# Delta-rule inverses ordered behind weight splits on DVE, and gates taken out of PSUM with one operation per head

## The chip, the cores and the metric

One core of a Trainium2 chip runs the kernel. Its engines work side by side, each through its own queue in order, and they meet through semaphores: PE (TensorE, matmuls out of SBUF into PSUM), DVE (VectorE), ACT (ScalarE), POOL (GpSimd), and SP, which here issues most DMAs. The metric is the time of one execution on the device in microseconds (us), the median of several.

## The reference: a decoder layer with two token mixers

The input x is 256 tokens by 2048 channels, in 32-bit floats. The layer is

```python
h = rmsnorm(x, norm_mix_w)
q, k, v, z, b_raw, a_raw, p_in, g_a, g_b = split(h @ w_in)
q, k, v = split(silu(causal_dwconv(concat(q, k, v), conv_qkv_w)))   # q, k l2-normalised per head
o = gated_delta_rule(q, k, v, g_log, beta)                          # 16 heads of 128, in chunks
y_a = rmsnorm(o, gdn_norm_w) * silu(z)
y_b = (causal_multiscale_pool(p_in) @ pool_w) * pool_scale
x = x + (sigmoid(g_a) * y_a + sigmoid(g_b) * y_b) @ w_out
h = rmsnorm(x, norm_ffn_w)
gate, up = split(h @ w_up)
x = x + (gelu(causal_dwconv(gate, conv_ffn_w) + conv_ffn_b) * up) @ w_down
y = rmsnorm(x, norm_final_w)
```

In the delta rule each chunk solves a unit lower triangular system, (I + L) u = rhs, with L made of products of the keys, decays and beta. The kernel uses chunks of 128 tokens, two per head, and inverts I + L.

## The kernel before

**Weights.** All weights (some 300 MB) stream through once, in tiles of 256 by 512 that are listed beforehand in `srcs` and taken in that order. `load` issues a tile's DMA on SP into one of four `raw` buffers. `begin` splits it into two parts that PE multiplies at its fast 32-bit rate: ACT casts `whi` (L141), DVE subtracts to get `wlo` (L149), three buffers each. `weights()` hands out the next tile and makes sure that the splits of the two tiles after it are in the program too (AHEAD = 2). `gemm_a` (L168) multiplies with one tile after another: for each, 12 matmuls of 512 columns (L179 high by high, L180 low by high, L181 high by low, for two halves of the tile and two blocks of tokens), into a `psm` buffer of PSUM. After each half tile it calls `side()`, which runs one step of a generator of side work. At its second tile it first runs what waits in the list `later`.

**The mixers, group by group.** The loop at L836 runs over four groups of four heads. Each multiplies in turn with K, Q, V, P (pooling input), GB (gate of the pooling branch), two tiles of pool, Z (the silu gate) and GA (gate of the delta branch); K, Q, V, P, GB, Z and GA have 8 tiles each. Group 0's K is done by hand earlier. In the second tile of V the generator `gdn` (L625) is started for the group. Its parts, with their yields:

- decays and their masks (4 yields); keys by keys and queries by keys, with the sums for the norms, giving `ga0` and `ga1` (8 yields);
- the 32 by 32 blocks on the diagonal of L go out by DMA to DRAM (`cdd`, L703) and come back spread over all partitions as `lb` (L706; 1 yield);
- WAIT = 5 empty yields, then a copy of the identity to `tb` (L715) and the inverse of all blocks, 31 columns with two dependent DVE operations each (L718, L720), a yield after every third column. Below, this is the chain of the inverse;
- `tb` goes to DRAM and back as the blocks of `TTa` (L725, L728); then what is left of `conv`, the convolution of the values (L594 to L600); ACT scales the values (L734);
- `qx`, `qp`: sums over the squared queries (L737, L740); transposes of the blocks (L745); the blocks are joined to 64 and 128 (U, px; L758 to L787); then products with the values: `w1`, `pr`, `w2` and the outputs `po`, two PSUM banks of the `psg` buffers, of which there are four (L793 to L811);
- the norm of the outputs: `pn` spreads the sums of the queries by a matmul (L814), four small DVE operations bring it to `ro` (L824); squares and sums of `po` (L819, L820); a power on POOL (L827); a factor (L829); and `on` = `po` times `ro` (L832), handed on in `res`.

At the end of a group `gated` (L901) runs the generator dry, multiplies `on` into `sz`, the product of the gates (L903), and adds `yb`, the pooling branch (L904). `mixed` (L913) transposes `sz` on PE (L224) and splits it into `mhi` (ACT, L916) and `mlo` (DVE, L917), the left side of the output projection. Groups 0 to 2 do `mixed` in the next group's K. Group 3 has its own order: 6 tiles of each of the first two column blocks of `w_out` are multiplied first, with what the groups 0 to 2 gave (`early`, L927); then come `gated` and `mixed`, and then the rest of the projection.

**What sets the order.** The program text gives each instruction its place. A planner then orders each engine's instructions with a clock of its own: an engine that is free takes, of the instructions that are ready by that clock, the one earliest in the text. So an instruction whose inputs are there early can run long before its place in the text, and one whose inputs come late in that clock is passed by others. On the chip each engine then goes through its order strictly, and waits at an instruction whose inputs are late in fact, with everything behind it. `tc.issue_after(ins)` forces what is inside to stand behind `ins` on the same engine.

Of the kernel before, what the change touches and what calls it, by code (L numbers as in the profile page):

```python
# [7 lines left out]
F32 = mybir.dt.float32  # L8
# [3 lines left out]
ALU = mybir.AluOpType  # L12

P = 128
# [6 lines left out]
EPS = 1e-6  # L21
# [6 lines left out]
NR = P // B0  # L28
AHEAD = 2
WAIT = 5  # L30


@with_exitstack
def kernel(
# [20 lines left out]
    nc = tc.nc  # L55
    mm = nc.tensor.matmul
# [10 lines left out]
    def nm(s):  # L67
        cnt[0] += 1
        return f"{s}_{cnt[0]}"

    def pg(shape=(P, 512)):
        return psg.tile(list(shape), F32, tag="g", name=nm("psg"))
# [33 lines left out]

    loads = []
    last_load = [None]
    HALVES = 2

    def weights(ahead=AHEAD):
# [21 lines left out]
    def begin(n):  # L133
        while len(made) < min(len(srcs), n):
            load(len(made) + 1)
            raw = loads[len(made)]
            shape = list(raw.shape)
            keep = kept.get(len(made))
            hi = wpool.tile(shape, F32R, tag="whi", name=nm("whi")) if keep is None else \
                mtile(keep, shape, F32R, nm("khi"))  # L140
            nc.scalar.copy(hi, raw)  # L141
            if shape[1] == 8:
                lo = None
                nc.vector.tensor_tensor(hi[:, :, 32:64], raw[:, :, 0:32], hi[:, :, 0:32].bitcast(F32),
                                        op=ALU.subtract)
            else:
                lo = wpool.tile(shape, F32R, tag="wlo", name=nm("wlo")) if keep is None else \
                    mtile(4 + keep, shape, F32R, nm("klo"))
                nc.vector.tensor_tensor(lo, raw, hi.bitcast(F32), op=ALU.subtract)  # L149
            made.append((hi, lo))  # L150


# [96 lines left out]
    mp = mix.__enter__()  # L249
# [66 lines left out]
    with tc.manual_schedule(engines={mybir.EngineType.PE, mybir.EngineType.DVE, mybir.EngineType.Activation}):  # L316
# [4 lines left out]
        n = 0  # L321
        for c in range(HALVES):
            for k in range(2):
# [108 lines left out]
    idb = mp.tile([P, 8, B0], F32, name="idb")  # L432
    for cq in range(4):
        pr = slice(32 * cq, 32 * cq + 32)
# [8 lines left out]
    for g, w in enumerate(WINDOWS):  # L443
# [11 lines left out]
    sel = mp.tile([P, 4, 32], F32, name="sel")  # L455
    nc.vector.tensor_reduce(sel[:, 0, :], ident.rearrange("p (b i) -> p i b", b=4), axis=mybir.AxisListType.X,
                            op=ALU.add)
# [4 lines left out]
    for c in range(2):  # L462
        hi, lo = weights()
# [161 lines left out]
    def gdn(g, kq, vt, conv, res):  # L625
# [6 lines left out]
        dec0 = mp.tile([P, 4, S], F32, tag="dec0", name=nm("dec0"))  # L632
# [31 lines left out]
        for hp in range(2):  # L664
            h0 = 2 * hp
            hs = slice(h0, h0 + 2)
            grams = []
            for h in (h0, h0 + 1):
# [5 lines left out]
                for t, src in ((0, pg0[:, 0:P]), (1, pg1[:, 0, :])):  # L674
                    nc.vector.tensor_tensor_reduce(jk, src, ident, scale=1.0, scalar=0.0, op0=ALU.mult,
                                                   op1=ALU.add, accum_out=ssk[:, t, h : h + 1])
# [6 lines left out]
            for h in (h0, h0 + 1):  # L683
# [4 lines left out]
                                               op0=ALU.mult, op1=ALU.mult)  # L688
# [3 lines left out]
                                               op0=ALU.mult, op1=ALU.mult)  # L692
# [15 lines left out]

        q2 = kq[:, :, 1, :]
        nc.scalar.activation(q2, q2, AF.Square)  # L710
        for _ in range(WAIT):
            yield
        tb = mp.tile([P, 8, B0], F32, tag="tb", name=nm("tb"))
        tmp = mp.tile([P, 8, B0], F32, tag="tmp", name=nm("tmp"))
        nc.vector.tensor_copy(tb, idb)  # L715
        for j in range(B0 - 1):
            tv = tmp[:, :, j + 1 :]
            nc.vector.tensor_tensor(tv, lb[:, j, j + 1 :].unsqueeze(1).to_broadcast([P, 8, B0 - 1 - j]),  # L718
# [13 lines left out]
        for h in range(4):  # L732
            for t in range(2):
# [5 lines left out]
        qp = mp.tile([P, 32], F32, tag="qp", name=nm("qp"))  # L739
        nc.vector.tensor_reduce(qp, qx.rearrange("p h (c j) -> p (h c) j", j=32), axis=mybir.AxisListType.X,  # L740
                                op=ALU.add)
        yield
        for r in range(NR):
            rs = slice(B0 * r, B0 * (r + 1))
            nc.vector.transpose(Ta[rs, :, rs], TTa[rs, :, rs])  # L745
# [27 lines left out]
        lo, up = slice(0, 64), slice(64, 128)  # L773
# [22 lines left out]
        pr = pg([P, 4, P])  # L796
# [9 lines left out]
        po = [pg([P, 4, P]) for t in range(2)]  # L806
# [3 lines left out]
            mm(po[1][:, h, :], ga0[:, h, 384:512], w1[:, h, :], start=True, stop=False)  # L810
            mm(po[1][:, h, :], ga1[:, h, P : 2 * P], w2[:, h, :], start=False, stop=True)  # L811
        yield
        pn = pg([P, 4, 2, 4])
        mm(pn.rearrange("p h t c -> p (h t c)"), sel.rearrange("p b i -> p (b i)"), qp, start=True, stop=True)  # L814
        ro = mp.tile([P, 2, 4], F32, tag="ro", name=nm("ro"))
        so = mp.tile([P, 2, 4], F32, tag="so", name=nm("so"))
        for t in range(2):
            o2 = mp.tile([P, 4, P], F32, tag="dec1", name=nm("o2"))
            nc.scalar.activation(o2, po[t], AF.Square, scale=float(P) ** -0.5)  # L819
            nc.vector.tensor_reduce(so[:, t, :], o2, axis=mybir.AxisListType.X, op=ALU.add)  # L820
        yield
        for c in range(4):
            pr = slice(32 * c, 32 * c + 32)
            nc.vector.tensor_scalar(ro[pr], pn[pr, :, :, c].rearrange("p h t -> p t h"), EPS * P, EPS * EPS * P,  # L824
                                    op0=ALU.mult, op1=ALU.add)
        nc.vector.tensor_tensor(ro, ro, so, op=ALU.add)
        nc.gpsimd.tensor_tensor(ro, ro, epsx[:, 0:1].unsqueeze(2).to_broadcast([P, 2, 4]), op=ALU.pow)  # L827
        for t in range(2):
            nc.vector.tensor_scalar(ro[:, t, :], ro[:, t, :], rsq[:, t : t + 1], None, op0=ALU.mult)  # L829
        on = mp.tile([P, 2, 4, P], F32, tag="dec0", name=nm("on"))  # L830
        for t in range(2):
            nc.vector.tensor_tensor(on[:, t], po[t], ro[:, t, :].unsqueeze(2).to_broadcast([P, 4, P]), op=ALU.mult)  # L832
        yield
        res.append(on)

    for g in range(4):  # L836
        kq = mp.tile([P, 4, 2, S], F32, tag="kq", bufs=1, name=nm("kq"))
# [7 lines left out]
        res = []  # L845
# [41 lines left out]
        tb = gate(gemm_a(xh, xl, KD), "th")  # L887
        ps = gemm_a(lambda k, t: phi[:, k, t * P : (t + 1) * P], lambda k, t: plo[:, k, t * P : (t + 1) * P], 4)
        yb = mp.tile([P, 2, 512], F32, tag="yb", name=nm("yb"))
# [4 lines left out]
        sz = mp.tile([P, 2, 512], F32, tag="sz", name=nm("sz"))  # L894
# [5 lines left out]

        def gated(sz=sz, res=res, yb=yb):  # L901
            drain()
            nc.vector.tensor_tensor(sz, res[0].rearrange("p t h d -> p t (h d)"), sz, op=ALU.mult)  # L903
            nc.vector.tensor_tensor(sz, sz, yb, op=ALU.add)  # L904

        if g < 3:
            gated()
# [31 lines left out]
    for c in range(4):  # L939
# [9 lines left out]
        for k2 in range(2):  # L949
# [5 lines left out]
            for kk in range(2):  # L955
# [4 lines left out]
                                               op0=ALU.mult, op1=ALU.subtract)  # L960
# [134 lines left out]
```

## Time and profile before

| | us |
|---|---|
| median of 3 runs | 1572.16 (1571.49 to 1575.03) |
| profiled execution | 1572.57 |
| its span, first to last instruction | 1570.8 |
| mixers, groups 0 to 3, end of Q/K of group 0 to the end of GA | 36 to 730 |
| output projection | 730 to 830 |
| gated MLP, first product | 830 to 1330 |
| its second product and the end | 1330 to 1570.8 |

TensorE's granted clock was 0.998 over the span. Timeline rows below have the start in us, the length in us, the engine, the line, the operation, what it writes and reads with shapes, how many are merged, and in brackets the idle time of the engine just before with what ended it. Rows of the page's groups have the line, the operation, shapes and count, then busy us and the mean ns of one, then idle time before them. Rows of waits have who waited for whom, the total us, how often, and the longest. A stretch's row has its length, then for PE, weight loads, DVE, ACT and POOL the busy us with the count, then clock, DMA share and GB/s.

### The profile page before, as it was taken

The page shows a single profiled execution, that of the slowest core. Times are in us where ns is not written, and L with a number is a line of the kernel's source. Part 1 is how long each engine was busy: PE and PEld are TensorE (multiplying, and loading weights), DVE is VectorE, ACT ScalarE, POOL GpSimd, SP SyncE. Part 2 cuts the span into 40 slices and gives each one's busy share as a digit, 9 for nine tenths or more (in the row PEclk, how much of TensorE's full clock was granted, in tenths as well). Part 3 has the DMA queues.
Part 4 walks back from the last instruction along what each step waited for, and adds up shares of the span by engine and source line. Part 5 has one row for each costly group of instructions (what it writes and reads, how often), then busy time and mean ns, then how long its engine had stood idle before and what let it go on. Part 6 is the DMA issues. An engine that isn't in the chain of part 4 may idle for free.

```text
span 1570.8 us, 21247 instructions
## 1 busy us (share of the span) xinstructions
PE 1558.3 (99%) x8022; PEld 1308.1 (83%) x8022; DVE 1077.4 (69%) x1647; ACT 744.7 (47%) x956; POOL 47.4 (3%) x69
## 2 busy tenths in 40 slices
PE   9999999999999999999999999999999999999997
PEld 8878888888887888888888888888888888888886
DVE  6897849796797758796656667766666667444444
ACT  6554446444554445544454544444444445334443
POOL 2110000000010001000000000000000000000000
PEclk9999999999999999999999999999999999999999
DMA  8676747666666756775555556555555566556662
GB/s 272 199 219 194 207 148 218 201 207 176 183 211 185 210 159 192 214 205 177 198 191 183 188 189 190 188 189 187 187 189 188 188 188 216 198 190 208 203 223 90
DMA packets 168229, 304.23 MB, mean 194 GB/s; under 512 B 19234, under 2 KB 22834, under 8 KB 167998
## 3 DMA queue, kind: packets, MB, share of 16 engines
q1 hardware_dynamic: 165104, 297.84, 61.0%
q10 hardware_dynamic: 3022, 5.03, 0.9%
q8 instruction: 63, 1.03, 0.3%
q14 instruction: 40, 0.33, 0.1%
HBM read 297.56 MB, written 5.27 MB: 193 GB/s over the span
## 4 chain that ended last, share of the span: by engine, by line
PE 50%; issue 1%; ACT 0%; DVE 0%; POOLq 0%; POOL 0%
PE psm L203 10%; PE psg L203 10%; PE psg L204 5%; PE psm L204 5%; PE psg L1008 2%; PE psg L1010 2%; PE psg L1009 2%; PE psm L1010 2%; PE psm L1008 2%; PE psm L1009 2%; PE psm L180 1%; PE psm L181 1%; PE psm L179 1%; PE psg L954 0%; ACT xt L1037 0%
## 5 line engine op out<-in xcount | busy, mean ns | idle before, releaser
L149 DVE TENSOR_TENSOR wlo<-raw,whi 128x1024 fp32r<-128x1024 f32 x522 | 636.9, 1222 | 379.2 <-ACT whi L141 373.6
L141 ACT CAST whi<-raw 128x1024 fp32r<-128x1024 f32 x524 | 550.8, 1053 | 715.1 <-PE psm L180 305.7
L181 PE MATMUL psm<-wlo,xhl 128*128 128x512 f32 x864 | 340.3, 394 | 1.1 <-DVE wlo L149 1.1
L179 PE MATMUL psm<-whi,xhl 128*128 128x512 f32 x864 | 339.6, 393 | 0.0
L180 PE MATMUL psm<-whi,xhl 128*128 128x512 f32 x864 | 338.2, 391 | 0.0
L203 PE MATMUL psm<-fhl,whi 128*128 128x512 f32 x704 | 246.2, 396 | 0.0
L203 PE MATMUL psg<-fhl,whi 128*128 128x512 f32 x704 | 238.0, 394 | 0.0
L204 PE MATMUL psm<-fhl,wlo 128*128 128x256 f32 x704 | 194.4, 279 | 0.0
L181 PEld LDWEIGHTS psm<-wlo,xhl 128*128 128x128 f32 x864 | 162.3, 188 | 34.8 <-DVE wlo L149 1.9
L180 PEld LDWEIGHTS psm<-whi,xhl 128*128 128x128 f32 x864 | 162.3, 188 | 33.2
L179 PEld LDWEIGHTS psm<-whi,xhl 128*128 128x128 f32 x864 | 162.3, 188 | 33.0 <-issue 0.5
L204 PE MATMUL psg<-fhl,wlo 128*128 128x256 f32 x704 | 178.7, 279 | 0.0
L203 PEld LDWEIGHTS psm<-fhl,whi 128*128 128x128 f32 x704 | 131.4, 188 | 30.5
L203 PEld LDWEIGHTS psg<-fhl,whi 128*128 128x128 f32 x704 | 129.2, 188 | 24.2
L204 PEld LDWEIGHTS psg<-fhl,wlo 128*128 128x128 f32 x704 | 132.5, 188 | 6.9
L204 PEld LDWEIGHTS psm<-fhl,wlo 128*128 128x128 f32 x704 | 132.5, 188 | 1.1
L1008 PE MATMUL psg<-whi,hhi 128*128 128x512 f32 x168 | 65.5, 390 | 0.0
L1008 PE MATMUL psm<-whi,hhi 128*128 128x512 f32 x168 | 65.4, 389 | 0.0
L1009 PE MATMUL psm<-whi,hlo 128*128 128x512 f32 x168 | 65.4, 389 | 0.0
L1010 PE MATMUL psm<-wlo,hhi 128*128 128x512 f32 x168 | 65.4, 389 | 0.0
L1009 PE MATMUL psg<-whi,hlo 128*128 128x512 f32 x168 | 65.4, 389 | 0.0
L1010 PE MATMUL psg<-wlo,hhi 128*128 128x512 f32 x168 | 59.1, 389 | 0.0
(263 smaller groups left out, 1527.2 us busy)
## 6 DMA issues: line engine op xcount, KB each, us to landing
raw<-in_w_in_dram SPq DMA_DIRECT2D x224, 512.0 KB, 4.2
raw<-in_w_up_dram SPq DMA_DIRECT2D x176, 512.0 KB, 4.6
raw<-in_w_down_dram SPq DMA_DIRECT2D x88, 512.0 KB, 4.3
raw<-in_w_out_dram SPq DMA_DIRECT2D x32, 512.0 KB, 3.7
mv<-vrow SPq DMA_DIRECT2D x12, 512.0 KB, 5.8
taps<-in_conv_qkv_w_dram SPq DMA_DIRECT2D x16, 256.0 KB, 5.6
raw<-in_pool_w_dram SPq DMA_DIRECT2D x8, 512.0 KB, 5.3
vrow<-ev SPq DMA_DIRECT2D x4, 512.0 KB, 3.1
```

Source lines behind the costliest of these rows:

```text
L141: nc.scalar.copy(hi, raw)
L149: nc.vector.tensor_tensor(lo, raw, hi.bitcast(F32), op=ALU.subtract)
L179: mm(ps[:, t, :], lh(k, t), hi[:, kk, :], start=(k == 0), stop=False)
L180: mm(ps[:, t, :], ll(k, t), hi[:, kk, :], start=False, stop=False)
L181: mm(ps[:, t, :], lh(k, t), lo[:, kk, :], start=False, stop=(k == nk - 1))
L203: mm(ps[f], hi[:, kk, fs], rhl(k), start=(k == 0), stop=False, skip_group_check=True)
L204: mm(ps[f][:, 1, :], lo[:, kk, fs], rhl(k)[:, 0, :], start=False, stop=(k == nk - 1), skip_group_check=True)
L1008: mm(acc[c][t], lh(k, t), hi[:, kk, :], start=(k == 0), stop=False)
L1009: mm(acc[c][t], ll(k, t), hi[:, kk, :], start=False, stop=False)
L1010: mm(acc[c][t], lh(k, t), lo[:, kk, :], start=False, stop=(k == KF - 1))
```

## The change

Three things are done. The copy that opens the inverse is put behind the newest weight split that the text has made at that point (`last_split`), and comes 26, 24, 22 or 18 calls of `side()` later in the text, by group, with all of the generator that follows it. The matmul `pn` and its four operations move from behind `po` to behind `qp`. And `on` is gone: `gated` multiplies `po` in PSUM into `sz` (two operations), then for each of eight pairs of head and token block one operation multiplies by the factor `ro` and adds `yb`.

```diff
@@ -28,6 +28,7 @@
 NR = P // B0
 AHEAD = 2
 WAIT = 5
+LATE = (26, 24, 22, 18)
 
 
 @with_exitstack
@@ -106,6 +107,7 @@
 
     loads = []
     last_load = [None]
+    last_split = [None]
     HALVES = 2
 
     def weights(ahead=AHEAD):
@@ -146,7 +148,7 @@
             else:
                 lo = wpool.tile(shape, F32R, tag="wlo", name=nm("wlo")) if keep is None else \
                     mtile(4 + keep, shape, F32R, nm("klo"))
-                nc.vector.tensor_tensor(lo, raw, hi.bitcast(F32), op=ALU.subtract)
+                last_split[0] = nc.vector.tensor_tensor(lo, raw, hi.bitcast(F32), op=ALU.subtract).ins
             made.append((hi, lo))
 
 
@@ -708,11 +710,13 @@
 
         q2 = kq[:, :, 1, :]
         nc.scalar.activation(q2, q2, AF.Square)
-        for _ in range(WAIT):
+        for _ in range(WAIT + LATE[g]):
             yield
         tb = mp.tile([P, 8, B0], F32, tag="tb", name=nm("tb"))
         tmp = mp.tile([P, 8, B0], F32, tag="tmp", name=nm("tmp"))
-        nc.vector.tensor_copy(tb, idb)
+
+        with tc.issue_after(last_split[0]):
+            nc.vector.tensor_copy(tb, idb)
         for j in range(B0 - 1):
             tv = tmp[:, :, j + 1 :]
             nc.vector.tensor_tensor(tv, lb[:, j, j + 1 :].unsqueeze(1).to_broadcast([P, 8, B0 - 1 - j]),
@@ -740,6 +744,13 @@
         nc.vector.tensor_reduce(qp, qx.rearrange("p h (c j) -> p (h c) j", j=32), axis=mybir.AxisListType.X,
                                 op=ALU.add)
         yield
+        pn = pg([P, 4, 2, 4])
+        mm(pn.rearrange("p h t c -> p (h t c)"), sel.rearrange("p b i -> p (b i)"), qp, start=True, stop=True)
+        ro = mp.tile([P, 2, 4], F32, tag="ro", name=nm("ro"))
+        for c in range(4):
+            pr = slice(32 * c, 32 * c + 32)
+            nc.vector.tensor_scalar(ro[pr], pn[pr, :, :, c].rearrange("p h t -> p t h"), EPS * P, EPS * EPS * P,
+                                    op0=ALU.mult, op1=ALU.add)
         for r in range(NR):
             rs = slice(B0 * r, B0 * (r + 1))
             nc.vector.transpose(Ta[rs, :, rs], TTa[rs, :, rs])
@@ -810,28 +821,18 @@
             mm(po[1][:, h, :], ga0[:, h, 384:512], w1[:, h, :], start=True, stop=False)
             mm(po[1][:, h, :], ga1[:, h, P : 2 * P], w2[:, h, :], start=False, stop=True)
         yield
-        pn = pg([P, 4, 2, 4])
-        mm(pn.rearrange("p h t c -> p (h t c)"), sel.rearrange("p b i -> p (b i)"), qp, start=True, stop=True)
-        ro = mp.tile([P, 2, 4], F32, tag="ro", name=nm("ro"))
         so = mp.tile([P, 2, 4], F32, tag="so", name=nm("so"))
         for t in range(2):
             o2 = mp.tile([P, 4, P], F32, tag="dec1", name=nm("o2"))
             nc.scalar.activation(o2, po[t], AF.Square, scale=float(P) ** -0.5)
             nc.vector.tensor_reduce(so[:, t, :], o2, axis=mybir.AxisListType.X, op=ALU.add)
         yield
-        for c in range(4):
-            pr = slice(32 * c, 32 * c + 32)
-            nc.vector.tensor_scalar(ro[pr], pn[pr, :, :, c].rearrange("p h t -> p t h"), EPS * P, EPS * EPS * P,
-                                    op0=ALU.mult, op1=ALU.add)
         nc.vector.tensor_tensor(ro, ro, so, op=ALU.add)
         nc.gpsimd.tensor_tensor(ro, ro, epsx[:, 0:1].unsqueeze(2).to_broadcast([P, 2, 4]), op=ALU.pow)
         for t in range(2):
             nc.vector.tensor_scalar(ro[:, t, :], ro[:, t, :], rsq[:, t : t + 1], None, op0=ALU.mult)
-        on = mp.tile([P, 2, 4, P], F32, tag="dec0", name=nm("on"))
-        for t in range(2):
-            nc.vector.tensor_tensor(on[:, t], po[t], ro[:, t, :].unsqueeze(2).to_broadcast([P, 4, P]), op=ALU.mult)
-        yield
-        res.append(on)
+        yield
+        res.append((po, ro))
 
     for g in range(4):
         kq = mp.tile([P, 4, 2, S], F32, tag="kq", bufs=1, name=nm("kq"))
@@ -900,8 +901,14 @@
 
         def gated(sz=sz, res=res, yb=yb):
             drain()
-            nc.vector.tensor_tensor(sz, res[0].rearrange("p t h d -> p t (h d)"), sz, op=ALU.mult)
-            nc.vector.tensor_tensor(sz, sz, yb, op=ALU.add)
+            po, ro = res[0]
+            for t in range(2):
+                nc.vector.tensor_tensor(sz[:, t, :], po[t].rearrange("p h d -> p (h d)"), sz[:, t, :], op=ALU.mult)
+            for t in range(2):
+                for h in range(4):
+                    hs = slice(h * P, (h + 1) * P)
+                    nc.vector.scalar_tensor_tensor(sz[:, t, hs], sz[:, t, hs], ro[:, t, h : h + 1], yb[:, t, hs],
+                                                   op0=ALU.mult, op1=ALU.add)
 
         if g < 3:
             gated()
```

## The prediction

> **What bounds the kernel now.** First the busy shares of the page, then the waits of PE.
>
> ```profile
> span 1570.8 us, 21247 instructions
> PE 1558.3 (99%) x8022; PEld 1308.1 (83%) x8022; DVE 1077.4 (69%) x1647; ACT 744.7 (47%) x956; POOL 47.4 (3%) x69
> ```
> ```profile
> PE psm L181 <- DVE wlo L149: 2.1, 2, 1.1
> PE psm L240 <- POOL ones L230: 1.1, 1, 1.1
> PE psm L180 <- DVE mlo L917: 0.6, 1, 0.6
> PE psm L179 <- ACT mhi L916: 0.5, 1, 0.5
> ```
>
> PE sets the time: its idle time is 1570.8 - 1558.3 = 12.5 us, and its recorded waits for other engines are 4.3 us in five pieces. One (1.1 us) is the start. The other four are all that work on DVE and ACT can give back: two waits for a weight split (L149) and two where the last group's gated values enter the output projection (L916, L917). So the question is whether the change takes away these four, and whether it makes others. The next view is PE's timeline at the four.
>
> ```profile
> 136.01 0.39 PE L179 MATMUL psm<-whi,phi 128*128 128x512 f32 x1
> 136.24 0.39 PE L180 MATMUL psm<-whi,plo 128*128 128x512 f32 x1
> 137.64 0.50 PE L181 MATMUL psm<-wlo,phi 128*128 128x512 f32 x1 [1.01 <-DVE wlo L149]
> ...
> 491.80 0.39 PE L180 MATMUL psm<-whi,xhl 128*128 128x512 f32 x1
> 493.30 0.50 PE L181 MATMUL psm<-wlo,xhl 128*128 128x512 f32 x1 [1.11 <-DVE wlo L149]
> ...
> 769.96 1.03 PE L224 MATMUL psg<-ident,sz 128*128 128x128 f32 x8
> 771.51 0.74 PE L179 MATMUL psm<-whi,mhi 128*128 128x512 f32 x2 [0.52 <-ACT mhi L916]
> 772.89 0.50 PE L180 MATMUL psm<-whi,mlo 128*128 128x512 f32 x1 [0.64 <-DVE mlo L917]
> 773.23 0.39 PE L181 MATMUL psm<-wlo,mhi 128*128 128x512 f32 x1
> ```
>
> The starts say more than the busy time: undisturbed, one 512-column matmul starts 0.23 us after the one before (136.01 to 136.24), so a weight tile of 12 matmuls takes PE about 2.72 us; I call that a step. At 137.64 the start is 137.64 - 136.24 - 0.23 = 1.17 us late, at 493.30 it is 1.27 us late. At the junction behind the transposes (L224) the waits are 0.52 us and then 773.23 - 771.51 - 3 x 0.23 = 1.03 us. [...]
>
> **What makes the two splits late.** DVE and ACT around these places:
>
> ```profile
> 128.90 1.23 DVE L149 TENSOR_TENSOR wlo<-raw,whi 128x1024 fp32r<-128x1024 f32 x1 [0.92 <-ACT whi L141]
> 136.03 0.42 DVE L718 TENSOR_TENSOR tmp<-lb,tb 128x248 f32<-128x248 f32 x1 [5.91 <-DMA lb<-cdd]
> 136.37 1.22 DVE L149 TENSOR_TENSOR wlo<-raw,whi 128x1024 fp32r<-128x1024 f32 x1
> ...
> 484.46 1.23 DVE L149 TENSOR_TENSOR wlo<-raw,whi 128x1024 fp32r<-128x1024 f32 x1 [0.69 <-ACT whi L141]
> 491.69 0.42 DVE L718 TENSOR_TENSOR tmp<-lb,tb 128x248 f32<-128x248 f32 x1 [6.00 <-DMA lb<-cdd]
> 492.02 1.22 DVE L149 TENSOR_TENSOR wlo<-raw,whi 128x1024 fp32r<-128x1024 f32 x1
> ```
> ```profile
> 130.54 1.05 ACT L141 CAST whi<-raw 128x1024 fp32r<-128x1024 f32 x1 [1.68 <-PE psm L180]
> 133.26 1.05 ACT L141 CAST whi<-raw 128x1024 fp32r<-128x1024 f32 x1 [1.67 <-PE psm L180]
> ...
> 486.10 1.05 ACT L141 CAST whi<-raw 128x1024 fp32r<-128x1024 f32 x1 [1.68 <-PE psm L180]
> ```
>
> In groups 0 and 2 the first product of the inverse (L718) stands on DVE in front of a split and waits 5.91 and 6.00 us until lb has landed. The cast that the split needs was done at 131.59 and 487.15, but the split runs at 136.37 and 492.02. In groups 1 and 3 the same wait is shorter and PE shows nothing:
>
> ```profile
> 313.33 0.42 DVE L718 TENSOR_TENSOR tmp<-lb,tb 128x248 f32<-128x248 f32 x1 [4.62 <-DMA lb<-cdd]
> ...
> 660.76 1.23 DVE L149 TENSOR_TENSOR wlo<-raw,whi 128x1024 fp32r<-128x1024 f32 x1 [1.42 <-ACT whi L141]
> 667.14 0.42 DVE L718 TENSOR_TENSOR tmp<-lb,tb 128x248 f32<-128x248 f32 x1 [3.60 <-DMA lb<-cdd]
> ```
>
> So DVE may stand still for 4.62 us and PE notices nothing; at 5.91 us it costs 1.17. That is the slack against which every new wait on DVE is held.
>
> **The change part by part.**
>
> *The tie (L715).* The copy that opens the inverse now follows the newest split. Which one that is comes from counting yields. Before the copy lie 4 + 8 + 1 yields and then 5 + LATE, so the copy is reached in call 14 + 5 + LATE: 45, 43, 41, 37. V's product gives 14 calls (the generator starts at its second tile), P's 16, GB's 16 at two per tile. So the copy is reached in tile 7, 6, 5 and 3 of GB. Splits are made two tiles ahead, so the tie is to the split of pool tile 1, pool tile 0, GB tile 7, GB tile 5. Counting the L149 rows by tile, the last split ahead of the first L718 is now GB 7, GB 6, GB 6, GB 5. The tie thus moves two, two, one and no splits in front of the chain.
>
> Group 0: the split of pool 0 can run from 131.59 to 132.8 and that of pool 1 from 133.26 + 1.05 = 134.31 to 135.5; the copy (292 ns) ends at 135.8 and L718 finds lb at 136.03. Both splits fit in the time that DVE stood still, and the chain starts no later. The 1.17 us go. Group 2: GB 7's split runs from 487.15 to 488.4 and L718 then waits until 491.69, 3.3 us, under the 4.62 that PE did not feel. The 1.27 us go. Group 1: pool 0's split ends at about 314.2, so L718 starts some 1 us later than 313.33, hidden. Group 3: nothing moves. Sum -2.44 us; with the idle times alone instead of the starts it would be -2.12.
>
> ```profile
> L715 DVE COPY tb<-idb 128x256 f32<-128x256 f32 x4 | 1.2, 292 | 3.0 <-DMA tbd<-tb 2.5 <-POOL idb L435 0.5
> L824 DVE TENSOR_SCALAR ro<-psg 32x8 f32<-32x8 f32 x16 | 2.6, 162 | 7.2 <-PE psg L814 7.1
> ```
>
> The copy no longer runs ahead into the previous group, where it held DVE 3.0 us in all for the stores of tb; it now adds 0.29 us in front of each chain, inside the waits above.
>
> *What LATE moves in the order of the program.* Behind the copy all of the inverse, the rest of conv (L594 to L600) and the tail stand later in the program by 18 to 26 calls, each half a step. The planner starts what is ready, though, and the rows show that it is the landing of lb, not the place in the program, that starts the chain: group 1's chain was due at call 19 (P tile 2) and ran at 313.33, in GB. DMAs behind it on SP (tbd, TT, and the weight loads between them) are tied to the chain's end, which does not move by more than the 1 us above. I cost this at nothing, with the bound of one step (2.72) on each side of a hand-over to PE as the rival prices it.
>
> *The norm's part (L813 to L825).* One matmul and four small operations per group move up behind qp; their number stays. L824 now waits for PE at another place; the 7.1 us of four groups are 1.8 us a time, below the slack of 4.62. Cost nothing.
>
> *The gates.* These rows carry the prices:
>
> ```profile
> L832 DVE TENSOR_TENSOR on<-psg,ro 128x512 f32<-128x512 f32 x8 | 5.2, 687 | 0.1
> L903 DVE TENSOR_TENSOR sz<-on,sz 128x1024 f32<-128x1024 f32 x4 | 4.9, 1219 | 0.0
> L904 DVE TENSOR_TENSOR sz<-sz,yb 128x1024 f32<-128x1024 f32 x4 | 4.9, 1224 | 0.1
> L600 DVE SCALAR_TENSOR_TENSOR vt<-th,vt 128x1024 f32<-128x1024 f32 x4 | 4.9, 1218 | 0.0
> L981 DVE SCALAR_TENSOR_TENSOR y<-gs,cfw,y 128x255 f32<-128x255 f32 x44 | 19.2, 477 | 0.0
> L675 DVE CUSTOM_DVE_ANT_0 jk<-psg,ident 128x128 f32<-128x128 f32 x32 | 9.2, 287 | 4.1 <-PE psg L670 2.3 <-PE psm L181 0.5
> ```
>
> Removed per group: 2 x 0.687 + 1.219 + 1.224 = 3.82 us. Added: two products out of PSUM, 2 x 0.687 = 1.37, and eight operations on 128 columns. No row has that form. Below stands L675 (287 ns, same width), above L981 (477 ns, 255 columns); the line through L981 and L600 has 0.963 ns a column and gives 477 - 127 x 0.963 = 355 ns, which I take. Eight are 2.84 us (2.30 to 3.82), the gates 4.21 us, so DVE has 0.4 us more per group (-0.15 to +1.37). It lies beside PE's wide matmuls: DVE is idle for 180.2 - 139.0 = 41 us of group 1.
>
> ```profile
> 187.50:367.70 180.20, 180.20 (x914) 148.10 (x912) 138.96 (x240) 86.84 (x118) 6.88 (x7) 1.00 0.66 196
> ```
>
> [...]
>
> Where cover is thin is the junction, in group 3:
>
> ```profile
> 764.00 0.35 DVE L829 TENSOR_SCALAR ro<-ro,rsq 128x4 f32<-128x4 f32 x2
> 767.97 1.22 DVE L904 TENSOR_TENSOR sz<-sz,yb 128x1024 f32<-128x1024 f32 x1
> 771.01 1.23 DVE L149 TENSOR_TENSOR wlo<-raw,whi 128x1024 fp32r<-128x1024 f32 x1 [0.67 <-ACT whi L141]
> ```
>
> From 764.00 to 769.19 the factor, on, one split and both gate operations run. After the change it is the factor (0.35), eight operations (2.84) and that split (1.2), 4.4 us against 5.2, since the two products out of PSUM need no factor and can run while POOL raises to the power. The gate ends 0.8 us earlier. But the transposes at 769.96 show no wait for sz: they stand behind the last early wide matmul in the order of the program. PE then waits for ACT to copy the transposes and for L917, which stands behind the split at 771.01. Neither starts earlier for an earlier gate. So I take 0 here, with -1.55 (0.52 + 1.03) and +1.6 (an equal wait for sz) as bounds.
>
> **Sum.** The profiled execution took 1572.57 us with a span of 1570.8, 0.4 above the median 1572.16 of the runs. 1572.57 - 1.17 - 1.27 + 0 = 1570.1 us. Own range 1568.9 to 1571.7: 1.2 below (most of the junction) and 1.6 above.
>
> **Rivals.**
>
> A, more goes than the two splits: the earlier gate lets the planner put L917 in front of the split at 771.01, or the transposes in front of the last early matmuls, and both waits of the junction go too: 1570.13 - 1.55 = 1568.6. For it: the gate ends 0.8 us earlier. Against it: the transposes did not wait for it.
>
> B, the tie is without effect: the wait for lb takes its place behind other splits and the next split is late instead by the same time, or the planner already had this order in its own clock. 1572.3, the time of before. For it: in group 3 the tie moves nothing. Against it: in group 0 both splits end before lb lands.
>
> C, slower: the tail of group 3 slides in PE's order. Its last part goes from PE to ACT or DVE and back three times (w1, pr, w2 with po), and each time waits in PE's queue among wide matmuls. The program now has it 18 calls later and the gates behind splits; if each hand-over misses its place by one step, the gate ends 3 x 2.72 = 8.2 us later. Decisive is the slack between 769.19 and 769.96, 0.77 us: beyond it every microsecond is PE's. 1570.13 + 8.16 - 0.77 = 1577.5; with two hand-overs 1574.8. For it: PE has nothing to do in place of these matmuls, and order is what the planner decides with its own clock. Against it: group 3's tie binds nothing and its chain starts with lb as before.
>
> **How the numbers follow.** A measurement of this kernel can tell about 0.2%, 3.1 us, from no change: faster is below 1569.0, slower above 1575.3. Forecast 0.47, of which 0.07 lies below 1569.0; A 0.25, nearly all below; B 0.10; C 0.18, of which 0.16 lies above 1575.3 (a tail that slides by less stays inside). Faster 0.31, same 0.53, slower 0.16. The range goes from 1567.8 (A with half a microsecond of side matmuls better placed) to 1576.0 (between C's two and three hand-overs), which leaves out about 0.17.
>
> **What would show it.** Right: no wait of PE for L149 in groups 0 and 2, first L718 behind the splits of pool 1, pool 0 and GB 7, its wait for lb under 1, 1 and 4 us; sums of 4.2 us a group for the gates, and the waits for L916 and L917 still there. Wrong: a new wait of PE for a split or at L916 of several microseconds (C), the two waits still there with the old order (B), or the sums in place and the time unmoved, which would mean that PE's side matmuls cost more in their new places.

## The result and the profile after

The changed kernel takes 1574.32 us (median of 22 runs, 1573.62 to 1576.16) against 1571.89 us before (22 runs, 1570.54 to 1575.03): 1.0016 of the time before, 95% interval 1.0010 to 1.0022. It is slower by some 2.4 us, where a gain of 2.4 us was forecast. The span of the profiled execution grew by less, 1.8 us, from 1570.8 to 1572.6, since the profiled execution of the kernel before (1572.57 us) lies 0.7 us above its median.

Waits of PE in the kernel after (who waited for whom, total us, how often, longest):

```profile
PE psg L226 <- DVE sz L910: 3.0, 2, 2.8
PE psm L242 <- POOL ones L232: 1.1, 1, 1.1
PE psm L312 <- ACT whi L132: 0.4, 1, 0.4
PE psm L183 <- DVE wlo L151: 0.2, 1, 0.2
```

The two waits for a split are gone (2.1 us before, 0.2 now, and that one elsewhere). In their place PE waits at the transposes of group 3 for `sz`, where it did not wait before. PE's timeline of the kernel after at that place:

```profile
767.49 0.39 PE L183 MATMUL psm<-wlo,mhi 128*128 128x512 f32 x1
770.66 0.30 PE L226 MATMUL psg<-ident,sz 128*128 128x128 f32 x1 [2.79 <-DVE sz L910]
771.19 1.65 PE L226 MATMUL psg<-ident,sz 128*128 128x128 f32 x7 [0.22 <-DVE sz L910]
772.89 1.22 PE L181 MATMUL psm<-whi,mhi 128*128 128x512 f32 x2
773.91 0.63 PE L182 MATMUL psm<-whi,mlo 128*128 128x512 f32 x1
774.34 0.63 PE L183 MATMUL psm<-wlo,mhi 128*128 128x512 f32 x1
...
776.00 0.39 PE L181 MATMUL psm<-whi,mhi 128*128 128x512 f32 x1
```

PE comes here at 767.49 + 0.23 = 767.72, 2.24 us earlier than before (769.96): so much the tie gave. Then it waits 2.79 us, and behind the wait the matmuls start 0.43 us apart instead of 0.23. The stretches of the kernel after say why (length, busy us and count of PE, weight loads, DVE, ACT, POOL, then the granted clock):

```profile
765.00:770.00 5.00, 2.88 (x18) 2.19 (x16) 3.28 (x6) 1.64 (x2) 1.64 (x1) 1.00 0.32 110
772.00:774.00 2.00, 1.95 (x8) 1.23 (x8) 1.49 (x4) 1.17 (x2) 0.00 (x0) 0.63 0.42 155
774.00:776.00 2.00, 2.00 (x7) 1.56 (x6) 0.19 (x1) 0.00 (x0) 0.00 (x0) 0.52 0.83 229
776.00:778.00 2.00, 2.00 (x10) 1.66 (x9) 0.00 (x0) 0.65 (x1) 0.00 (x0) 1.00 1.03 358
```

The granted clock falls to about half after the wait and is back at 776. It isn't this execution alone: the mean clock is 0.996 or 0.997 in all 22 executions of the changed kernel, and 0.998 or 0.999 in all those of the kernel before that ran beside the experiments below. The third column block of the projection begins at 786.11, before it was 784.25. So from the end of the early products to that point PE needs 786.11 - 767.72 = 18.39 us against 14.29 before: 4.10 more, less the 2.24 won, is 1.86 us, the span's growth (1.8). The 4.10 are 770.66 - 767.72 = 2.94 us until the first transpose, 0.68 us in the transposes, which take 2.23 us instead of 1.55 since `sz` comes piece by piece, and 0.48 us behind them, where the stretch up to the third column block takes 786.11 - 772.89 = 13.22 us instead of 784.25 - 771.51 = 12.74.

Why `sz` is late is seen on DVE. The first product of the inverse in groups 0, 2 and 3 of the kernel after:

```profile
135.96 0.42 DVE L722 TENSOR_TENSOR tmp<-lb,tb 128x248 f32<-128x248 f32 x1
...
490.50 0.42 DVE L722 TENSOR_TENSOR tmp<-lb,tb 128x248 f32<-128x248 f32 x1 [0.64 <-DMA lb<-cdd]
...
668.83 0.42 DVE L722 TENSOR_TENSOR tmp<-lb,tb 128x248 f32<-128x248 f32 x1 [1.81 <-DMA lb<-cdd]
```

The wait for `lb` is gone in group 0, as forecast; 0.64 us are left of 6.00 in group 2, and 1.81 of 3.60 in group 3. But the inverses take longer. From the first to the last operation, read off the timelines, they took 39.8, 40.0, 40.1 and 38.3 us, and now take 44.4, 44.3, 43.8 and 42.7. Groups of DVE within group 0's inverse, first of the kernel before and then of the kernel after (busy us, mean ns, then idle before them and its cause):

```profile
L149 DVE TENSOR_TENSOR wlo<-raw,whi 128x1024 fp32r<-128x1024 f32 x16 | 19.5, 1219 | 0.1
```
```profile
L151 DVE TENSOR_TENSOR wlo<-raw,whi 128x1024 fp32r<-128x1024 f32 x16 | 19.6, 1224 | 2.9 <-ACT whi L143 2.8
L602 DVE SCALAR_TENSOR_TENSOR vt<-th,vt 128x1024 f32<-128x1024 f32 x1 | 1.2, 1219 | 0.0
```

The same sixteen splits stand in it. Before, they were late: each cast was long done when DVE came to the split. Now they are on time, DVE stands before them until the cast is there (2.9 us in all), and the inverse behind waits with it. Further, the values' last operation (L602, 1.2 us) now falls into the inverse; before it was done ahead of it. In groups 1 and 2 it is the same: 2.3 us of idle time before the splits in each, 0.2 and 0.3 before the change. In group 3 the idle time grew less, from 0.5 to 1.3 us; there one more split and an operation of the silu gate (L896) fall into the inverse as well, some 1.2 us each.

### The profile page after: what moved, and what is told of

The parts are those of the page before. It is cut to its first block, busy times and chain, and to the rows that moved or that the text cites. A ratio compares the mean times of both kernels' runs of the same rounds, so it can differ in the third digit from the quotient of the medians.

```text
span 1572.6 us, 21271 instructions
## 1 busy us (share of the span) xinstructions
PE 1559.6 (99%) x8022; PEld 1308.8 (83%) x8022; DVE 1078.0 (69%) x1671; ACT 745.6 (47%) x956; POOL 44.6 (3%) x69
## 4 chain that ended last, share of the span: by engine, by line
PE 97%; DMA 1%; issue 1%; DVE 1%; ACT 0%; SPq 0%; POOLq 0%; POOL 0%; DVEq 0%
PE psm L183 15%; PE psm L181 15%; PE psm L182 15%; PE psm L205 10%; PE psg L205 10%; PE psg L206 5%; PE psm L206 5%; PE psg L1015 2%; PE psg L1016 2%; PE psg L1017 2%; PE psm L1016 2%; PE psm L1015 2%; PE psm L1017 2%; PE psm L312 1%; PE psg L672 1%
## 5 line engine op out<-in xcount | busy, mean ns | idle before, releaser
L206 PE MATMUL psg<-fhl,wlo 128*128 128x256 f32 x704 | 178.8, 279 | 0.0
```

The source lines that it names most:

```text
L206: mm(ps[f][:, 1, :], lo[:, kk, fs], rhl(k)[:, 0, :], start=False, stop=(k == nk - 1), skip_group_check=True)
```

## The experiments

Two theories stand against each other. T: the tie makes `sz` late, by the longer inverses. G: the new gates make it late, by their many small operations.

To compare kernels whose PE is ahead or behind, I count PE's progress in weight tiles: 12 wide matmuls each, from group 0's Q on, taken from the starts in the timelines. The transposes of group 3 stand behind tile 236. The table has, for each kernel, when group 2's gates end, when group 3's `ga` begins, when its inverse begins and ends, all in tiles, and PE's wait for `sz` in us.

| kernel | gates 2 end | ga 3 begins | inverse 3 | wait for sz | median us | ratio, 95% |
|---|---|---|---|---|---|---|
| before | 179.8 | 191.2 | 202.1 to 216.2 | 0 | 1571.89 | 1 |
| after | 181.4 | 197.2 | 203.6 to 219.2 | 3.0 | 1574.32 | 1.0016 (1.0010 to 1.0022) |
| gates_only | 177.4 | 190.2 | 201.6 to 215.3 | 0 | 1573.79 | 1.0013 (1.0004 to 1.0022) |
| tie_only | 181.8 | 197.2 | 203.7 to 219.2 | 6.4 | 1576.75 | 1.0029 (1.0017 to 1.0040) |
| g3_free | 181.4 | 197.2 | 203.8 to 219.0 | 2.0 | 1574.00 | 1.0014 (1.0005 to 1.0022) |
| late_no_tie | 177.4 | 190.2 | 201.4 to 216.1 | 0 | 1571.75 | 0.9999 (0.9990 to 1.0008) |
| tie_g0 | 178.8 | 190.3 | 201.4 to 215.3 | 0 | 1571.17 | 0.9997 (0.9988 to 1.0006) |
| tie_g3 | 177.4 | 190.2 | 202.0 to 218.2 | 0.2 | 1573.25 | 1.0011 (1.0002 to 1.0020) |
| conv_first | 179.8 | 191.2 | 202.0 to 218.0 | 0.9 | 1571.17 | 0.9997 (0.9989 to 1.0006) |
| after_fill | 181.4 | 197.2 | 203.6 to 219.2 | 0.2 | 1573.28 | 1.0008 (0.9999 to 1.0017) |
| conv_g012 | 179.8 | 191.2 | 201.6 to 216.2 | 0 | 1570.37 | 0.9991 (0.9982 to 1.0000) |
| conv_g02 | 179.8 | 191.2 | 201.5 to 216.2 | 0 | 1569.80 | 0.9987 (0.9978 to 0.9996) |
| conv_g02_old | 180.8 | 197.2 | 203.6 to 219.0 | 6.3 | 1577.28 | 1.0036 (1.0022 to 1.0050) |

Each ratio is to runs of the kernel before on the same chip; these had medians of 1571.4 to 1572.1 us, so the ratio is what compares kernels of different rows. `ga` comes in two halves, and the inverse needs both: the last of it ends at tile 200.1 in the five kernels with 197.2 in the table, at 197.4 to 198.4 in the others. So of a beginning that is six tiles later about 1.7 tiles reach the inverse.

**gates_only.** The changed kernel without tie and later place:

```diff
-LATE = (26, 24, 22, 18)
+LATE = (0, 0, 0, 0)
-        with tc.issue_after(last_split[0]):
-            nc.vector.tensor_copy(tb, idb)
+        nc.vector.tensor_copy(tb, idb)
```

> The gates and the norm's part as changed, the inverse as before (no tie, no later place). Theory T (the loss is group 3's inverse, which is put later, so that sz is late at the transposes; the gates are harmless): group 3's inverse ends near 705 us as before, PE has no wait for sz, the two waits for a weight split near 137 and 493 us are there again: 1571 to 1572.5 us, no difference from before. Theory G (the eight small operations per group make sz late): a wait of 2 to 3 us for sz at the transposes of the junction, 1574 to 1575 us.

PE's waits in it:

```profile
PE psm L183 <- DVE wlo L151: 2.6, 3, 1.2
PE psm L182 <- DVE mlo L923: 0.6, 1, 0.6
PE psm L181 <- ACT mhi L922: 0.5, 1, 0.5
```

No wait for `sz`, and the two waits of the junction as before: the eight small operations don't make `sz` late, so theory G falls. The waits for splits are three and not two, and at other places, near 311, 490 and 655 us. The time is higher than theory T had it, with a wide spread (1571.99 to 1576.97 us; the profiled execution took 1573.07). By the time alone the gates could be blamed, 1.0013 here against 1.0016; but late_no_tie and tie_g0 have the same gates and are at 0.9999 and 0.9997. What the executions near 1576 us lose isn't in the profile of one near 1573, and stays open; their mean clock, 0.997 or 0.998, is about that of the others (0.998 or 0.999).

**tie_only.** The kernel before with `LATE` and the tie, as in the change's diff, and the old gates and norm.

> The tie and the later place as changed, the gates and the norm's part as before. Theory T: both waits for splits are gone (-2.4 us), the wait for sz at the junction is there (about 3 us, and PE slow for some us behind it): 1573.5 to 1575.5 us. Theory G: no wait for sz, 1569.5 us.

1576.75 us, above theory T's range, with a wait for `sz` of 6.4 us. So the tie costs more than the change as a whole, and the gates with the moved norm win back some of it: with otherwise the same tie, PE waits 3.0 us in the changed kernel.

**g3_free.** The changed kernel with group 3 as before:

```diff
-LATE = (26, 24, 22, 18)
+LATE = (26, 24, 22, 0)
+        if g < 3:
+            with tc.issue_after(last_split[0]):
+                nc.vector.tensor_copy(tb, idb)
+        else:
+            nc.vector.tensor_copy(tb, idb)
```

> As the changed kernel, but group 3 has neither the tie nor the later place. Theory T: both waits for splits gone, group 3's inverse ends earlier against PE than in the changed kernel, wait for sz at most 1 us: 1569 to 1570.5 us, the fastest. Theory G: the wait for sz stays, 1574 us.

A miss for theory T: 1574.0 us and a wait of 2.0 us, though group 3 has no tie of its own. The table shows what it inherits: `ga` of group 3 begins six tiles later than before and ends 1.7 later, and its inverse begins 1.7 tiles later.

**late_no_tie.** The later place alone: `LATE` as in the change, the copy without `issue_after`.

> As the changed kernel with the later place in the text, but the copy isn't tied to the split. Theory T leaves open which of the two delays group 3. If the place does: the wait for sz stays and the two waits for splits come back, 1576 to 1577 us. If the tie does: no wait for sz, the two waits for splits come back, 1571.5 to 1572.5 us. Theory G: wait for sz and waits for splits, 1576.5 us.

No wait for `sz`, two waits for splits (1.4 us), 1571.75 us: no difference from before that can be told. The place in the text alone does no harm (gates_only, which differs in the place alone, is at 1573.79); the tie, to the split that the later place selects, does.

**tie_g0 and tie_g3.** The changed kernel with tie and later place in one group only, `LATE = (26, 0, 0, 0)` or `(0, 0, 0, 18)`, and the plain copy where the number is 0.

> Gates and norm's part as changed; tie and later place in group 0 alone. Theory T (the tie makes a group's inverse end two to three weight tiles of PE later; only group 3 pays, because there PE has a slack of 0.77 us): group 0's inverse ends near PE's tile 48.3 instead of 46.2, without any wait of PE there; group 3 ends its gates before the transposes as in the kernel before; the wait near 137 us is gone: 1570 to 1571.5 us. Theory I (the delay is handed on from group to group): group 3's sz is late by 1 us or more, 1573 us or more.

> Gates and norm's part as changed; tie and later place in group 3 alone. Theory T: group 3's own tie delays its gates by one to three tiles against PE, a wait for sz of 2 to 4 us with PE's clock at half behind it, and the waits for splits in groups 0 to 2 stay: 1576 to 1578 us. Theory I: group 3 starts in time since nothing is handed on, no wait for sz: 1571.5 to 1573 us.

With group 0 alone tied its inverse ends at tile 48.3, as in the change (46.2 before), and nothing downstream is late: 1571.17 us. With group 3 alone tied its inverse takes 44.2 us, and group 3 starts in time. Its end is at tile 218.2, and the gates end almost in time: a wait of 0.2 us, not theory T's 2 to 4, and 1573.25 us, just above theory I's range. With the same gates the inverse of group 3 ends at tile 215.3 without any tie (gates_only), at 218.2 with its own alone, at 219.0 with those of the other groups alone (g3_free) and at 219.2 with all. So each of the two, its own tie and what is handed on, makes it late by about three tiles or more, and they don't add up. Neither theory had that. As in gates_only the spread is wide (1571.13 to 1577.07 us).

**conv_first.** The changed kernel, with what is left of the convolution ahead of the later place:

```diff
-        for _ in range(WAIT + LATE[g]):
+        for _ in range(WAIT):
+            yield
+        for _ in conv:
+            yield
+        for _ in range(LATE[g] - 5):
             yield
...
-        for _ in conv:
-            yield
         for h in range(4):
```

> As the changed kernel, but what is left of the values' convolution stands ahead of the later place and not behind the inverse; the copy and its tie stay in the same calls. If the values' last operation inside the chain (1.2 us, 0.45 tile) matters, all four chains are 1.2 us shorter and the wait for sz falls from 2.8 to about 1.6 us: 1572 to 1573.5 us. If the chain's length comes from DVE waiting for the casts alone, the chains stay at 43 to 44 us and the time at 1574.3 us.

1571.17 us, below both forecasts: 3.2 less than the changed kernel, and more than I expected from 1.2 us of DVE time. The inverses take 43.3 to 43.6 us, with 2.2 to 2.8 us of idle time before the splits, so most of the added length is the waiting for casts. The larger part of the gain is in what is handed on: group 2's gates end at tile 179.8 again, `ga` of group 3 begins at 191.2 again, and the wait for `sz` is 0.9 us, after which the clock stays at 1.00.

**after_fill.** The changed kernel with work for PE during its wait (its result is not used):

```diff
+    fill = pg()
+    with tc.issue_after(last_mm[0]):
+        for _ in range(12):
+            mm(fill, onesr, xhl[:, 0], start=True, stop=True)
```

> As the changed kernel, with twelve more matmuls of 512 columns (2.7 us of PE time, their result is not used) behind the early products, where PE waits for sz. If the halved clock behind that wait is a price of its own, of some 2.6 us, PE stays at full clock behind the junction and the kernel is faster though it does more: 1571.5 to 1572.5 us. If the wait alone is the loss, the time stays at 1574.3 us or rises.

With twelve added matmuls the kernel is at 1573.28 against 1574.32 us, above the 1571.5 to 1572.5 that were expected (ratios 1.0008 and 1.0016, whose intervals overlap, so the time alone doesn't show that it is faster). The profile is clearer: a wait of 0.2 us, a granted clock of 1.00 all through the junction. From the first matmul behind the transposes to the third column block PE takes 785.49 - 773.41 = 12.08 us instead of 786.11 - 772.89 = 13.22. The halved clock costs 1.1 us, less than the 2.6 I had expected. That the same stretch is only 0.48 us longer than before the change is due to the wait for `mlo` (0.64 us), which was in it before and is in neither of these two.

**conv_g012 and conv_g02.** conv_first with `LATE = (26, 24, 22, 0)` or `(26, 0, 22, 0)`, the tie only where the number isn't 0.

> As conv_first, but group 3's copy isn't tied and comes right behind the convolution. Theory T: group 3's splits are late again during its inverse, so the inverse is shorter by the 2 to 3 us that DVE waited for casts; its gates end before the transposes and the rest of the wait at the junction (0.95 us) goes: 1569.5 to 1570.7 us. If the inverse's length in group 3 doesn't depend on its own tie: 1571.2 us, as conv_first.

> As conv_first, but only groups 0 and 2, where PE waited for splits in the kernel before, have the tie. Theory T: both waits gone, group 3 in time: 1569.5 to 1570.7 us, and not slower than conv_g012. If untied groups bring new waits for splits, 0.5 to 1.5 us more: 1570.5 to 1572 us.

Both meet theory T: without its own tie group 3's inverse ends at tile 216.2 as before, the transposes don't wait, and no wait for a split is left. Theory T's reason holds in part: the inverse takes 39.7 and 39.8 us instead of 43.6 in conv_first, of which 1.3 us are waiting for casts (1.5 against 2.8); most of the rest is a split and an operation of the silu gate that no longer fall into it. DVE and PE of conv_g02 at the junction:

```profile
763.30 1.14 DVE L915 SCALAR_TENSOR_TENSOR sz<-sz,ro,yb 128x128 f32<-128x128 f32 x4
764.35 1.22 DVE L151 TENSOR_TENSOR wlo<-raw,whi 128x1024 fp32r<-128x1024 f32 x1
765.49 1.13 DVE L915 SCALAR_TENSOR_TENSOR sz<-sz,ro,yb 128x128 f32<-128x128 f32 x4
```
```profile
767.28 1.03 PE L226 MATMUL psg<-ident,sz 128*128 128x128 f32 x8
768.84 0.73 PE L181 MATMUL psm<-whi,mhi 128*128 128x512 f32 x2 [0.52 <-ACT mhi L928]
770.21 0.50 PE L182 MATMUL psm<-whi,mlo 128*128 128x512 f32 x1 [0.64 <-DVE mlo L929]
```

The gates end at 766.62, 0.66 us ahead of the transposes, and PE is there 2.68 us earlier than before (767.28 against 769.96). The junction's own two waits remain, as forecast. conv_g02 is faster than both kernels. A second set of runs, on one chip with the next one:

> The same kernel as conv_g02 a second time, beside the one with the old gates on one chip: 1569.5 to 1570.3 us, 0.9982 to 0.9992 of the kernel before.

1569.78 us, 0.9988 (0.9980 to 0.9997): the same.

**conv_g02_old.** conv_g02 with the gates and norm of the kernel before.

> As conv_g02, with the gates and the norm's part of the kernel before. If the new gates and the moved norm shorten the tail of group 3 (tie_only against the changed kernel says by 3 to 4 us of the wait for sz), the old ones end after PE's last early product here: a wait for sz of 1 us or more, 1571 to 1573 us. If they only shift work on DVE without a use where the inverse is in time: 1569.8 us, as conv_g02.

1577.28 us: 7.5 us more than with the new gates, far above the 1571 to 1573 expected, and a wait for `sz` of 6.3 us. With the old gates group 2's end at tile 180.8 and not 179.8, `ga` of group 3 begins at 197.2, and all that follows is late. The new gates with the moved norm are thus what keeps group 2 in time here, though they were costed at nothing.

## Why the prediction was wrong

**The two waits for splits.** Right in place and size: the splits of pool 1, pool 0 and GB 7 go first, the chains of groups 0 and 2 find `lb` after 0 and 0.64 us, and PE comes to the junction 2.24 us earlier (2.44 forecast; a new wait of 0.2 us near 107 us is the difference). The count of splits ahead of the first L718, "GB 7, GB 6, GB 6, GB 5", was one too high in groups 2 and 3. PE's late matmul at 493.30 is the third of tile 146, which is GB 6 of group 2 counted from 0 as the prediction does; so the split at 492.02 is GB 6's, and the one ahead of L718 is GB 5's. Splits follow in the order of the tiles, and counting on from there the one ahead of L718 in group 3 is GB 4's. The tie thus moves two splits in group 2, which is why L718 waits 0.64 us there and not the forecast 3.3, and one, GB 5's, in group 3.

**The step that failed** is the sentence that what hangs on the inverse is "tied to the chain's end, which does not move by more than the 1 us above". It looked at the start of the inverse alone. The start did stay in groups 0 to 2, but the inverse became 4.3 us longer on average, (44.4 + 44.3 + 43.8 + 42.7 - 39.8 - 40.0 - 40.1 - 38.3) / 4. The wait for `lb` had a use: it made the splits late, and late splits find their casts done, so that DVE then worked through without a gap. The tie moves that idle time from in front of the inverse into it, where 31 dependent columns wait behind each split. late_no_tie, where splits and inverse keep their order, has inverses of 38.8 to 42.4 us though the values' last operation stands in them too, and 0.1 to 0.5 us of idle time before their splits. The two idle times go against each other in all kernels of the table: where DVE waited less than 0.8 us for `lb`, it stood 2.1 to 2.9 us before the splits of that inverse; where it waited more than 2.9 us, at most 0.9 us.

**"Group 3: nothing moves"** failed in two ways. Its own tie does move a split, and makes its inverse longer (tie_g3: 44.2 us, with 2.5 us of idle time before the splits; end at tile 218.2, with a start at 202.0). And it inherits from group 2 (g3_free: `ga` at 197.2). In the changed kernel its inverse begins 1.5 tiles later and is 1.6 tiles longer. In the 13 kernels the hand-on has a sharp edge: where group 2's gates end at tile 179.8 or earlier, group 3's `ga` begins at 190.2 to 191.2; where at 180.8 or later, at 197.2. It is DVE's order that differs there. The first sum of the keys (L675, now L677) comes at 630.66 before and at 630.73 after, one tile later by PE's count. Before, the other sums, `sj` and `ga` follow at once,

```profile
630.66 0.28 DVE L675 CUSTOM_DVE_ANT_0 jk<-psg,ident 128x128 f32<-128x128 f32 x1
...
632.42 0.17 DVE L679 TENSOR_SCALAR ssk<-ssk 128x4 f32<-128x4 f32 x1
632.63 0.18 DVE L681 RECIPROCAL sj<-ssk 128x4 f32<-128x4 f32 x1
633.11 0.75 DVE L685 SCALAR_TENSOR_TENSOR ga<-psg,sj,dec 128x512 f32<-128x512 f32 x1
```

and after, operations of the convolution and splits stand between them all:

```profile
630.73 0.29 DVE L677 CUSTOM_DVE_ANT_0 jk<-psg,ident 128x128 f32<-128x128 f32 x1 [0.77 <-PE psg L672]
...
642.22 0.17 DVE L681 TENSOR_SCALAR ssk<-ssk 128x4 f32<-128x4 f32 x1
642.28 1.22 DVE L151 TENSOR_TENSOR wlo<-raw,whi 128x1024 fp32r<-128x1024 f32 x1
643.42 1.22 DVE L597 TENSOR_TENSOR vt<-vt,mv 128x1024 f32<-128x1024 f32 x1
644.56 0.17 DVE L683 RECIPROCAL sj<-ssk 128x4 f32<-128x4 f32 x1
...
646.97 0.74 DVE L687 SCALAR_TENSOR_TENSOR ga<-psg,sj,dec 128x512 f32<-128x512 f32 x1
```

From the first sum to `ga` DVE took 633.11 - 630.66 = 2.45 us before and takes 646.97 - 630.73 = 16.24 us after. The convolution's work is then done, so the second half of `ga` loses less, 1.7 tiles in all. Which readiness in the planner's clock turns the order round wasn't tried and stays open.

**The gates.** The price was about right:

```profile
L910 DVE SCALAR_TENSOR_TENSOR sz<-sz,ro,yb 128x128 f32<-128x128 f32 x32 | 8.8, 346 | 0.0
L906 DVE TENSOR_TENSOR sz<-psg,sz 128x512 f32<-128x512 f32 x8 | 5.4, 680 | 0.0
L752 DVE TENSOR_SCALAR ro<-psg 32x8 f32<-32x8 f32 x16 | 2.6, 162 | 0.2
```

346 ns where 355 were estimated, and 680 where 687. The sum of single times overstates a row of small operations, since they overlap: the eight of the last group take 2.19 us from first start to last end, 0.27 us each, where 8 x 0.346 would be 2.77. So DVE has (8.8 + 5.4) / 4 = 3.55 us of gates per group against (5.2 + 4.9 + 4.9) / 4 = 3.75. What was wrong is the worth of nothing: with the same tie the old gates have PE wait 6.4 us, the new ones 3.0 (tie_only and after), and 6.3 against 0 in conv_g02_old and conv_g02. Without a tie the new gates let group 2's end at tile 177.4 instead of 179.8. That is 2.4 tiles for 0.2 us of DVE time, so it comes from the order, and whether from the gates or from the norm's part wasn't taken apart. The norm's operation (L752) also no longer stops DVE: 0.2 us of idle time ahead of it, 7.2 before. The forecast had this wait only move.

**The junction.** Taken as 0 with a bound of 1.6 us, it cost 4.1 us more than in the kernel before, by the wait for `sz` and the clock behind it: above the bound, since that was set by the waits seen before and not by how late `sz` could be. That the waits for `mhi` and `mlo` gain nothing from an earlier gate is right: conv_g02 has the gate 0.66 us ahead of the transposes and the same 0.52 and 0.64 us. So rival A's gain isn't there to be had by an earlier gate, and rival B, by which the waits for splits would stay, fell with them.

**The place in the text** (`LATE`) was costed at nothing and by itself cost nothing: late_no_tie is at 0.9999.

**Rival C** had the right sign, the right place and the deciding slack (0.77 us), but not the mechanism. No hand-over of the tail misses its place: from the end of group 3's inverse to the sums of its outputs (`so`) there are 15.3 tiles, 15.5 before. The inverse itself ends three tiles later. That C's 1574.8 us for two hand-overs lies near the measured 1574.3 is luck. Against C the prediction put that "group 3's tie binds nothing"; it binds GB 5's split, and tie_g3 shows what that does.

The 1.86 us lost are thus: 2.24 won at the splits; 2.94 paid waiting for `sz`, 0.68 in the slower transposes and 1.1 for the clock, less 0.6 to 0.7 for the wait for `mlo` that is gone. conv_g02, which takes the win and leaves out what made `sz` late, comes out at 0.9987 and 0.9988; the forecast gain of 2.44 us in 1572.57 would be 0.9984, inside both intervals, but for another kernel than the one it was made for.

## What to carry to other kernels

Before a wait is taken off an engine, look at what it covers: work that was late behind the wait finds its inputs done, and without the wait the engine may stop for them one at a time, possibly inside a dependent chain (DVE stood 0.1 us before the splits of group 0's inverse with the wait, and 2.9 us without it). Follow the moved work to the place where the consumer has least slack (here 0.77 us in the last group), and count its progress in the bounding engine's own steps, so that a consumer that comes earlier is seen too. Those steps also tell which item stands ahead of a wait; a count that was off by one hid that the last group's tie moved a split. Tie only those groups in which the tie removes a wait.

## What the runs showed of the hardware

TensorE's granted clock halved at the junction in the four kernels in which PE waited 1.80 us or more there for `sz`: the kernel after (2.79 us), g3_free (1.80), tie_only (6.4) and conv_g02_old (6.3). Stretches of the kernel after, first those in which the clock falls, then that in which it returns:

```profile
772.00:772.50 0.50, 0.50 (x5) 0.31 (x4) 0.36 (x2) 0.25 (x1) 0.00 (x0) 1.00 0.93 340
772.50:773.00 0.50, 0.45 (x3) 0.16 (x2) 0.13 (x1) 0.46 (x2) 0.00 (x0) 0.50 0.64 246
...
775.50:776.00 0.50, 0.50 (x3) 0.35 (x3) 0.00 (x0) 0.00 (x0) 0.00 (x0) 0.58 0.85 225
```

A mean of 0.58 in the last half microsecond is 0.42 us at half and 0.08 at full clock, so the low stretch goes from 772.5 to 775.92, 3.4 us. It begins 1.8 us after the wait of 2.79 us is over, while PE works. The same in g3_free, after a wait of 1.80 us:

```profile
772.00:772.50 0.50, 0.47 (x2) 0.30 (x2) 0.50 (x1) 0.50 (x1) 0.00 (x0) 0.97 0.00 0
772.50:773.00 0.50, 0.39 (x2) 0.00 (x0) 0.50 (x2) 0.00 (x1) 0.00 (x0) 0.50 0.00 0
```

In conv_first, with 0.95 us of wait at the same place, it stays at 1.00. In tie_only, with its wait of 6.4 us from 766.59 on, the low stretch is three times as long:

```profile
768.00:770.00 2.00, 0.00 (x0) 0.00 (x0) 1.97 (x5) 0.00 (x0) 0.00 (x0) 0.77 0.04 7
...
778.00:780.00 2.00, 2.00 (x7) 1.55 (x6) 0.00 (x0) 0.02 (x1) 0.00 (x0) 0.67 1.02 376
```

Worked out in the same way it goes from 769.08 to 779.32, 10.2 us. In conv_g02_old the clock was 0.66 from 772 to 774 us, 0.50 from there to 778 and 0.63 from 778 to 780, so the low stretch goes from 772.64 to 779.48, 6.8 us, after a wait of nearly the same length. The fall isn't tied to the wait's end: it came 1.8 us after it in the kernel after, 2.5 us into the wait in tie_only and some 5 us into it in conv_g02_old. From the last early wide matmul to the next wide one PE has 5.17 us in the changed kernel and 4.18 in g3_free, where the clock fell, and 2.60 in conv_first and 1.55 in the kernel before, where it didn't. But in tie_only the 2.5 us of wait ahead of the fall are less than the 2.60 of conv_first, so the length of that stretch alone doesn't decide. What sets the moment of the fall and the length of the low stretch isn't shown by these runs. The stretches of gates_only and tie_g3 show no fall; what their executions near 1576 us lose stays open, as said above.
